# Second block of a fused two-block kernel: every product that GpSimd computes there is given to VectorE

## The chip, the cores and the metric

The kernel runs on one core of one Trainium2 chip, in one launch. The metric is the device time of that launch in microseconds (us). The kernel before took 2101.74 us (median of three runs, 2098.4 to 2101.85).

Names: PE is TensorE (matrix products), DVE is VectorE, ACT is ScalarE, POOL is GpSimd, SP is SyncE, whose queue starts the loads of weights. ACTq and SPq are the queues in which ACT and SP start transfers or wait. "L106" is line 106 of the kernel before.

## The reference, cut to what matters

Two blocks follow each other on 256 tokens of width 2048, all in float32. The change touches the second alone, an RWKV-7 block with a gated short convolution:

```
hn = rmsnorm(concat(16 meta tokens, x));  P = hn @ w_in            # 272 x 2048 @ 2048 x 8320
r, k, v, g_r, wl, al = split(token_shift(P[:, :4224]))              # the recurrent half
Bg, Cg, hc, g_c     = split(P[:, 4224:])                            # the convolution half
a  = sigmoid(a0 + al @ a_lora_up);  decay = exp(-exp(w_raw(wl)))
kk = normalise(k * k_k);  k = k * (1 + (a - 1) * k_a)
y  = recurrence over tokens: S = S diag(decay) - (S kk)(kk*a)^T + v k^T,  y_t = S r_t
y_a = (groupnorm(y) + bonus(r, k, v)) * silu(g_r)
y_b = Bg * causal_conv(Cg * hc) * silu(g_c)
h   = h + concat(y_a, y_b) @ w_out;  out = rmsnorm(h)
```

## The kernel before, in words

**Weights.** All weights (345 MB) are streamed once, in chunks of 128 x 1024 floats (512 KB). A chunk is loaded by SP into one of three tiles `st` (L131). `split` then makes two float32r halves of it: ACT casts it to `wh` (L105), and `wl = st - wh` is computed by DVE or POOL (L106); each half has four tiles. A tile `st` is free for the next load when both halves are done. PE multiplies each chunk three times (hi x hi, hi x lo, lo x hi), so every chunk needs its cast, its subtraction and its PE work in turn. In the second block each third chunk has its subtraction on POOL (`share`, L149 and L150).

**Sections.** In the second block `feat_super` computes 512 features at a time over 16 input tiles, that is 8 chunks (a section); four PSUM accumulators (of six, tile `acc`) take the result. At the end of a section an `evac` function empties the four: DVE reads PSUM (L1095, L193, L1154, L1160), ACT and DVE finish the product. PE may begin the next section in the two accumulators that are left, then needs the emptied ones. The order of sections is k, low-rank inputs, r, v, g, g, then the convolution's Cg, hc, g_c, Bg; then k, r, v and the convolution for the second half of the features; then the output projection (`tok_super`), at first over the part of its inputs that is ready.

**Recurrence.** The generator `rwkv` does the recurrence of one half of the heads by chunks of 64 tokens. Between chunks of weights, `pump` lets it advance by 1.1 credits; each `yield` names what it has used. Its longest part is an elimination that inverts 72 triangular 32 x 32 blocks at once: 31 steps of one product (L1393, into `XT`) and one subtraction (L1397, into `X`) on DVE, one after the other. Then `X` goes to DRAM and comes back in another layout (L1406, L1408, L1413, all started in ACT's queue), and the chunk-by-chunk state update follows (L1509 to L1561), with a group norm (`group_norm`).

**What sets the order.** All engines work in order. A scheduler puts the instructions of each engine in a fixed order when the program is built, by its own estimates of time; a waiting instruction holds up all that stand behind it on its engine.

**What POOL does in the second block before.** Fills with constants (memsets), one small copy (L1338), a third of the subtractions of L106, and these products: gates (L1172, L1173, L1179, L1205), keys (L1256, L1257, L1280), decays (L1316, L1332, L1530) and a row product at the very end (L1659).

Of the kernel before, what the change touches and what calls it, by code (L numbers as in the profile page):

```python
# [9 lines left out]
F32 = mybir.dt.float32  # L10
# [3 lines left out]
ALU = mybir.AluOpType  # L14
AX = mybir.AxisListType

P = 128
D = 2048
S = 256
NM = 16  # L20
# [13 lines left out]
def bc(ap, n):  # L34
    return ap.unsqueeze(len(ap.shape)).to_broadcast(list(ap.shape) + [n])
# [8 lines left out]
def fused_two_blocks(  # L44
# [9 lines left out]
    pe, act, dve, pool = nc.tensor, nc.scalar, nc.vector, nc.gpsimd  # L54
# [18 lines left out]
    queue = []  # L73
# [26 lines left out]
    behind = [None]  # L100
    mm_last = [None]

    def split(hi, lo, src, eng=dve):
        return (
            act.copy(hi, src),  # L105
            eng.tensor_tensor(lo, src, hi.bitcast(F32), ALU.subtract),  # L106
        )

    AHEAD = 3
# [3 lines left out]
    splits = []  # L113
    hold = []
    spare = []
    pos = [0, 0]
# [9 lines left out]
    def load_chunk():  # L126
        w2, k0, nk, c0, ncol = plan[pos[0]]
        pos[0] += 1
        st = wpool.tile([P, WCH], F32, name="st", bufs=3)
        n = nk * ncol  # L130
        nc.sync.dma_start(  # L131
            st[:, :n].rearrange("p (k n) -> p k n", n=ncol),
            w2[k0 * P:(k0 + nk) * P, c0:c0 + ncol].rearrange("(k p) n -> p k n", p=P),
        )
        loaded.append((st[:, :n], ncol))

    def issue_chunk():
        if not loaded:
            load_chunk()
        st, ncol = loaded.pop(0)  # L140
        if spare:
            t = T(spare.pop(0), F32R)
            wh, wl = (t[:, i * WCH:i * WCH + st.shape[1]] for i in range(2))
        else:
            wh, wl = (wpool.tile([P, WCH], F32R, name=name)[:, :st.shape[1]] for name in ("wh", "wl"))
        with ExitStack() as es:
            while hold:
                es.enter_context(tc.issue_after(hold.pop().ins))
            share = behind[0] is not None and queue and pos[0] % 3 == 0  # L149
            splits.append(split(wh, wl, st, pool if share else dve))  # L150
        ready.append(tuple(w.rearrange("p (k n) -> p k n", n=ncol) for w in (wh, wl)))

    def next_chunk(k0, c0, ncol):
# [127 lines left out]
    def T(i, dt=F32):  # L281
        t = tpool.tile([P, 2048], dt, name=f"t{i}")
        return t
# [804 lines left out]
    def x_ops(t0):  # L1088
        return lambda k: xo[:, k, :, t0:]
# [43 lines left out]
    kT = k_proj(0, x_ops0, z_scr)  # L1133
# [7 lines left out]
    mixt = mixpool.tile([P, KT, S], F32, name="mixt")  # L1141
# [7 lines left out]
    def conv_half(hf):  # L1149
        u = rw.tile([P, 4, S + 2], F32, name="u")  # L1150
        n = S + 2

        def ev_c(i, ps):
            dve.tensor_tensor(u[:, i, :], ps, rr3[:, T14:], ALU.mult)  # L1154

        def ev_h(i, ps):
            z = rw.tile([P, L], F32, name="z", bufs=2)
            f = 4 * hf + i
            o = mixt[:, 8 + f, :]
            dve.tensor_tensor(z[:, :n], ps, rr3[:, T14:], ALU.mult)  # L1160
            dve.tensor_tensor(u[:, i, :], u[:, i, :], z[:, :n], ALU.mult)
            act.activation(o, u[:, i, 2:], AF.Copy, scale=pv("conv2", f))
            dve.scalar_tensor_tensor(o, u[:, i, 1:n - 1], pv("conv1", f), o, ALU.mult, ALU.add)
            dve.scalar_tensor_tensor(o, u[:, i, 0:n - 2], pv("conv0", f), o, ALU.mult, ALU.add)

        def ev_g(i, ps):
            z = rw.tile([P, L], F32, name="z", bufs=2)
            g = rw.tile([P, S], F32, name="g", bufs=2)
            o = mixt[:, 8 + 4 * hf + i, :]
            scaled(z[:, :S], ps, rr3[:, NM:])  # L1170
            act.activation(g, z[:, :S], AF.Sigmoid)
            pool.tensor_tensor(g, g, z[:, :S], ALU.mult)  # L1172
            pool.tensor_tensor(o, o, g, ALU.mult)  # L1173

        def ev_b(i, ps):
            g = rw.tile([P, S], F32, name="g", bufs=2)
            o = mixt[:, 8 + 4 * hf + i, :]
            scaled(g, ps, rr3[:, NM:])
            pool.tensor_tensor(o, o, g, ALU.mult)  # L1179

        base = 4224 + 512 * hf
        sec(base + 1024, T14, ev_c)
        sec(base + 2048, T14, ev_h)
        sec(base + 3072, NM, ev_g)
        sec(base, NM, ev_b)

# [12 lines left out]
    def g_proj(hf):  # L1199
        def ev(i, ps):  # L1200
            g = rw.tile([P, S], F32, name="g", bufs=2)
            f = 4 * hf + i
            ev_shift(mixt[:, f, :], 24 + f, ps, T14)
            act.activation(g, mixt[:, f, :], AF.Sigmoid)
            pool.tensor_tensor(mixt[:, f, :], mixt[:, f, :], g, ALU.mult)  # L1205
        sec(3072 + 512 * hf, T14, ev)

    def c64(t, pi):
# [2 lines left out]
    def rwkv(hf, kT, src):  # L1211
        f0 = 4 * hf
        ARm = rw.tile([P, 4, 32], F32, name="ARm")
        BKm = rw.tile([P, 4, 64], F32, name="BKm")
# [4 lines left out]
        aa = r4("a")  # L1219
        for j in range(4):  # L1220
            f = f0 + j
# [8 lines left out]
        kk = r4("kk")  # L1230
        tmp = r4("tmp")
# [14 lines left out]
        ein = r4("ein")  # L1246
# [6 lines left out]
        for j in range(4):  # L1253
            f = f0 + j
            dve.tensor_scalar(tmp[:, j, :], aa[:, j, :], pv("k_a", f), oka[:, f:f + 1], ALU.mult, ALU.add)
        pool.tensor_tensor(kT, kT, tmp, ALU.mult)  # L1256
        pool.tensor_tensor(aa, kk, aa, ALU.mult)  # L1257
        yield 1.3
        AR = rw.tile([P, 2, 4, 2, 2, 64], F32, name="AR")
        BK = rw.tile([P, 2, 4, 2, 2, 64], F32, name="BK")  # L1260
# [15 lines left out]
        for pi in range(2):  # L1276
            dve.tensor_tensor(BK[:, pi, :, :, pi, :], c64(aa[:, :, NM:], pi), c64(nm_, pi), ALU.mult)
            dve.tensor_tensor(BK[:, pi, :, :, 1 - pi, :], c64(kT[:, :, NM:], pi), c64(nm_, pi), ALU.mult)
            if pi == 0:
                pool.tensor_tensor(tmp[:, :, :S], tmp[:, :, :S], kT[:, :, NM:], ALU.mult)  # L1280
            yield 1.3
        dve.tensor_tensor(BKm[:, :, 0:NM], aa[:, :, :NM], eneg[:, :, :NM], ALU.mult)
        dve.tensor_tensor(BKm[:, :, 32:32 + NM], kT[:, :, :NM], eneg[:, :, :NM], ALU.mult)
# [5 lines left out]
        for pi in range(2):  # L1289
            for pp in range(2):  # L1290
                bs = [mix_bank(), mix_bank()]
                for i in range(4):
                    p, cp = 2 * pp + i // 2, i % 2
                    for h in range(2):
                        q = slice(64 * h, 64 * h + 64)
                        pe.matmul(
                            bs[h][:, i * P:(i + 1) * P],
                            BK[q, pi, p, cp].rearrange("p a t -> p (a t)"),
                            AR[q, pi, p, cp].rearrange("p a t -> p (a t)"),
                            start=True, stop=True,  # L1300
                        )
                for h in range(2):
                    dve.tensor_tensor(
                        SS[:, pi, 2 * pp:2 * pp + 2, :, h, :].rearrange("p a c t -> p (a c) t"),
                        bs[h].rearrange("p (a t) -> p a t", t=P), bc_mid(mk[:, pi, :], 4), ALU.mult,
                    )
                yield 1.3
            for g in range(2):
                r0 = 64 * pi + 32 * g
                blk = 16 * (2 * pi + g)  # L1310
                nc.scalar.dma_start(
                    nd[blk:blk + 16].rearrange("b s t -> s b t"),
                    SS[r0:r0 + 32, pi, :, :, :, r0:r0 + 32].rearrange("s p c h t -> s (p c h) t"),
                )

            pool.tensor_tensor(  # L1316
                BK[:, pi].rearrange("p a c s t -> p a c (s t)"), BK[:, pi].rearrange("p a c s t -> p a c (s t)"),
                c64(em, pi)[..., 63:64].to_broadcast([P, 4, 2, P]), ALU.mult,
            )
        for h in range(2):  # L1320
            q = slice(64 * h, 64 * h + 64)
# [7 lines left out]
        nc.scalar.dma_start(nd[64:72].rearrange("b s t -> s b t"), SSm[0:32])  # L1329
        X0 = r4("X0", tag="sw").rearrange("p a t -> p (a t)")[:72, :1024].rearrange("p (s t) -> p s t", t=32)  # L1330
        nc.scalar.dma_start(X0, nd)
        pool.tensor_tensor(BKm, BKm, ein[:, :, NM - 1:NM].to_broadcast([P, 4, 64]), ALU.mult)  # L1332
        decs = rw.tile([P, 4, 4], F32, name="decs")
        dve.tensor_copy(decs, em.rearrange("p a (c t) -> p a c t", t=64)[:, :, :, 63])
        yield 0.7
# [83 lines left out]
        Z = r4("Z", P, tag="kk")  # L1419
        Zd = r4("Zd", P, tag="tmp")  # L1420
# [33 lines left out]
        for i in range(8):  # L1454
            p, h = i // 2, i % 2
            q = slice(64 * h, 64 * h + 64)
# [3 lines left out]
        for h in range(2):  # L1460
            q = slice(64 * h, 64 * h + 64)
# [48 lines left out]
        for c in range(4):  # L1510
            cp, pi = c // 2, c % 2
            a, o = 64 * pi, 64 * (1 - pi)
# [14 lines left out]
            if c < 3:  # L1527
                for h in range(2):
                    q = slice(64 * h, 64 * h + 64)
                    pool.tensor_tensor(Zd[q, :, q], Z[q, :, q], bc(decs[q, :, c], 64), ALU.mult)  # L1530
            if c >= 2:
                next(norm0)
            yield
# [10 lines left out]
            if c < 3:  # L1544
                b4 = mix_bank().rearrange("p (a t) -> p a t", t=P)
                for p in range(4):
                    for h in range(2):
                        q = slice(64 * h, 64 * h + 64)
                        pe.matmul(b4[q, p, q], BKt[:, pi, p, cp, q], UV[:, pi, p, cp, q], start=True, stop=True)
                for h in range(2):  # L1550
                    q = slice(64 * h, 64 * h + 64)
# [33 lines left out]
    for h in range(2):  # L1585
        q = slice(64 * h, 64 * h + 64)
# [5 lines left out]
    for h in range(2):  # L1592
        q = slice(32 * h, 32 * h + 32)
# [7 lines left out]
    for hf in range(2):  # L1601
        if hf == 1:
            kT = k_proj(1, x_ops(0), lambda: None)
            drain()
        src = {}
# [78 lines left out]
    for tb in range(2):  # L1684
        for s in range(2, 4):
            a = acc_bank()
            for k in OUT2_KT:
                if k % 2 == 0 and tb == 0:
                    chunks[s, k] = next_chunk(k, 512 * s, 512)[1]
                wh, wl = (w[:, k % 2, :] for w in chunks[s, k - k % 2])  # L1690
                hi, lo = (mix_ops(k)[:, i, tb * P:(tb + 1) * P] for i in range(2))
# [37 lines left out]
```

## Time and profile before

| | |
|---|---|
| median of three runs | 2101.74 us |
| the profiled execution, its own time | 2102.48 us |
| its span (first to last instruction) | 2100.8 us |
| second block | from about 1485 us of the span to its end |
| PE busy, share of the span | 2050.6 us, 98% |
| DVE, ACT, POOL busy | 1236.1, 1039.0, 323.2 us |
| granted TensorE clock, mean | 0.992 |

Times in rows are us from the start of the span, durations of one instruction are ns. A row that says "idle before <-ACT wh L105" tells how long the engine stood idle in front of such instructions, and what ended the wait. PE's instructions overlap each other, so a stretch in which PE is 100% busy is one without a gap, and the busy times of its groups may not be added up.

### The profile page before, as it was taken

The numbers are of one execution on the slowest core, as the hardware profiler recorded it, in microseconds if no ns is written. First come the engines' busy times: TensorE is split into PE (matmuls) and PEld (weight loads), VectorE is DVE, ScalarE is ACT, GpSimd is POOL, SyncE is SP. The second block draws the span as 40 slices with busy tenths as digits, with TensorE's granted clock in tenths as the row PEclk, the third lists the DMA queues.
The fourth block names the chain that finished last, engine by engine and source line by source line (L and its number), as shares of the span: only waits on it lengthen the run. The fifth ranks groups of instructions, "written<-read, shape, count | busy, mean of one in ns | idle before, by whom it ended". The sixth has DMA issues, their size and how long they took to land.

```text
span 2100.8 us, 29559 instructions
## 1 busy us (share of the span) xinstructions
PE 2050.6 (98%) x11592; PEld 1753.3 (83%) x11592; DVE 1236.1 (59%) x1603; ACT 1039.0 (49%) x1426; POOL 323.2 (15%) x271
## 2 busy tenths in 40 slices
PE   8999999999999999999999999999899999999898
PEld 7898888888888878888888888888798988998686
DVE  6546668654565574444444455565776855668635
ACT  5456566564434464444444454554564434544444
POOL 7002014300011000000000000000034324243422
PEclk9999999999999999999999999999999999999999
DMA  7676654566655566666666655555555553455534
GB/s 223 174 195 184 171 171 141 151 200 192 208 192 180 191 180 192 184 190 190 191 190 189 190 180 187 187 188 190 171 142 167 157 159 104 148 165 165 175 132 141
DMA packets 187884, 369.00 MB, mean 176 GB/s; under 512 B 21229, under 2 KB 29616, under 8 KB 186960
## 3 DMA queue, kind: packets, MB, share of 16 engines
q1 hardware_dynamic: 174752, 352.43, 55.6%
q10 hardware_dynamic: 12016, 11.43, 1.8%
q0 software_dynamic: 976, 3.24, 0.4%
q8 instruction: 91, 1.49, 0.3%
q14 instruction: 49, 0.40, 0.1%
HBM read 361.67 MB, written 5.38 MB: 175 GB/s over the span
## 4 chain that ended last, share of the span: by engine, by line
PE 83%; DVE 8%; DMA 4%; ACT 2%; issue 2%; POOL 1%; ACTq 0%; SPq 0%; DVEq 0%; POOLq 0%
PE acc L221 19%; PE acc L222 19%; PE acc L223 19%; PE acc L177 8%; PE acc L178 4%; PE acc L182 3%; PE acc L183 3%; PE acc L184 3%; DVE wl L106 3%; DMA st<-in_w_in_dram 2%; DVE XT L1393 1%; ACT wh L105 1%; DVE X L1397 1%; PE mx L846 1%; PE mx L714 1%
## 5 line engine op out<-in xcount | busy, mean ns | idle before, releaser
L106 DVE TENSOR_TENSOR wl<-st,wh 128x1024 fp32r<-128x1024 f32 (+1 forms) x626 | 772.4, 1235 | 683.5 <-ACT wh L105 672.6
L105 ACT CAST wh<-st 128x1024 fp32r<-128x1024 f32 (+1 forms) x672 | 699.1, 1042 | 885.7 <-PE acc L222 582.2
L221 PE MATMUL acc<-wh,opnd 128*128 128x512 f32 (+1 forms) x1280 | 498.1, 390 | 4.1 <-ACT opnd L105 4.0
L222 PE MATMUL acc<-wh,opnd 128*128 128x512 f32 (+1 forms) x1280 | 493.4, 386 | 2.2 <-DVE opnd L106 1.7
L223 PE MATMUL acc<-wl,opnd 128*128 128x512 f32 (+1 forms) x1280 | 492.3, 385 | 0.0
L177 PE MATMUL acc<-opnd,wh 128*128 128x512 f32 x896 | 326.7, 406 | 3.2 <-DVE z L193 3.2
L221 PEld LDWEIGHTS acc<-wh,opnd 128*128 128x128 f32 x1280 | 240.8, 188 | 51.0 <-ACT opnd L105 4.2
L222 PEld LDWEIGHTS acc<-wh,opnd 128*128 128x128 f32 x1280 | 241.1, 188 | 48.1 <-DVE opnd L922 2.2
L223 PEld LDWEIGHTS acc<-wl,opnd 128*128 128x128 f32 x1280 | 240.8, 188 | 46.5
L178 PE MATMUL acc<-opnd,wl 128*128 128x256 f32 x896 | 253.0, 282 | 4.6 <-DVE wl L106 4.6
L182 PE MATMUL acc<-opnd,wh 128*128 128x258 f32 (+1 forms) x784 | 225.8, 293 | 4.3 <-DVE z L1095 3.0
L183 PE MATMUL acc<-opnd,wh 128*128 128x258 f32 (+1 forms) x784 | 226.1, 290 | 0.0
L184 PE MATMUL acc<-opnd,wl 128*128 128x258 f32 (+1 forms) x784 | 225.0, 288 | 0.3 <-POOL wl L106 0.3
L177 PEld LDWEIGHTS acc<-opnd,wh 128*128 128x128 f32 x896 | 170.2, 190 | 43.3 <-DVE z L193 3.9
L178 PEld LDWEIGHTS acc<-opnd,wl 128*128 128x128 f32 x896 | 171.0, 191 | 6.1 <-DVE wl L106 5.9
L106 POOL TENSOR_TENSOR wl<-st,wh 128x1024 fp32r<-128x1024 f32 x46 | 118.6, 2578 | 267.2 <-ACT wh L105 244.2
L182 PEld LDWEIGHTS acc<-opnd,wh 128*128 128x128 f32 x784 | 148.5, 191 | 8.8 <-DVE z L1095 3.4
L183 PEld LDWEIGHTS acc<-opnd,wh 128*128 128x128 f32 x784 | 149.7, 191 | 1.6 <-issue 1.4
L184 PEld LDWEIGHTS acc<-opnd,wl 128*128 128x128 f32 x784 | 149.4, 191 | 1.4 <-POOL wl L106 0.5
L221 PE MATMUL acc<-wh,hh 128*128 128x512 f32 x352 | 138.7, 396 | 0.9 <-ACT hh L105 0.9
L222 PE MATMUL acc<-wh,hh 128*128 128x512 f32 x352 | 139.1, 395 | 0.0
L223 PE MATMUL acc<-wl,hh 128*128 128x512 f32 x352 | 138.9, 395 | 0.0
(434 smaller groups left out, 2057.5 us busy)
## 6 DMA issues: line engine op xcount, KB each, us to landing
st<-in_w_in_dram SPq DMA_DIRECT2D x290, 512.0 KB, 3.7
st<-in_w_ffn_in_dram SPq DMA_DIRECT2D x176, 512.0 KB, 3.7
st<-in_w_ffn_down_dram SPq DMA_DIRECT2D x88, 512.0 KB, 3.1
st<-in_w_o_dram SPq DMA_DIRECT2D x32, 512.0 KB, 3.6
st<-in_w_out_dram SPq DMA_DIRECT2D x32, 512.0 KB, 3.6
st<-in_w_in_dram SPq DMA_DIRECT2D x24, 344.0 KB, 3.6
st<-in_w_up_b_dram SPq DMA_DIRECT2D x16, 512.0 KB, 3.7
st<-in_w_up_a_dram SPq DMA_DIRECT2D x16, 512.0 KB, 3.9
```

The source lines that it names most:

```text
L105: act.copy(hi, src),
L106: eng.tensor_tensor(lo, src, hi.bitcast(F32), ALU.subtract),
L177: pe.matmul(av, wh[:, k, m:m + mw], pair, start=first, stop=False)
L178: mm_last[0] = pe.matmul(av[:, 1, :], wl[:, k, m:m + mw], pair[:, 0, :], start=False, stop=last)
L182: pe.matmul(av, wh[:, k, m:m + mw], pair[:, 0, :], start=first, stop=False)
L183: pe.matmul(av, wh[:, k, m:m + mw], pair[:, 1, :], start=False, stop=False)
L184: mm_last[0] = pe.matmul(av, wl[:, k, m:m + mw], pair[:, 0, :], start=False, stop=last)
L221: pe.matmul(a, hi, wk, start=j == 0, stop=False)
L222: pe.matmul(a, lo, wk, start=False, stop=False)
L223: mm_last[0] = pe.matmul(a, hi, wm, start=False, stop=j == nkt - 1)
L714: pe.matmul(b[:, h * P:(h + 1) * P], ke[:, h, ts], qe[:, h, ts], start=True, stop=True)
L846: pe.transpose(b[:, i * P:(i + 1) * P], src[:, i * P:(i + 1) * P], ident)
```

## The change

The argument that let `split` name an engine goes, and with it the rule by which a third of the chunks went to POOL: all subtractions of L106 are DVE's. All products of POOL in the second block but the row product at the end (L1659) go to DVE. In `ev_g` the factors are taken in another order: first z times the convolution's output (into z), then times sigmoid(z), so the first of the two needs no sigmoid. In `rwkv` a `yield 0.6` stands between the two products of the keys. Lines between 150 and 1256 stand one line higher in the changed kernel (its L1204 is L1205 of before, its L1094 is L1095).

```
-    def split(hi, lo, src, eng=dve):
+    def split(hi, lo, src):
...
-            eng.tensor_tensor(lo, src, hi.bitcast(F32), ALU.subtract),
+            dve.tensor_tensor(lo, src, hi.bitcast(F32), ALU.subtract),
...
-            share = behind[0] is not None and queue and pos[0] % 3 == 0
-            splits.append(split(wh, wl, st, pool if share else dve))
+            splits.append(split(wh, wl, st))
...
-            pool.tensor_tensor(g, g, z[:, :S], ALU.mult)
-            pool.tensor_tensor(o, o, g, ALU.mult)
+            dve.tensor_tensor(z[:, :S], z[:, :S], o, ALU.mult)
+            dve.tensor_tensor(o, z[:, :S], g, ALU.mult)
...
-            pool.tensor_tensor(o, o, g, ALU.mult)
+            dve.tensor_tensor(o, o, g, ALU.mult)
...
-            pool.tensor_tensor(mixt[:, f, :], mixt[:, f, :], g, ALU.mult)
+            dve.tensor_tensor(mixt[:, f, :], mixt[:, f, :], g, ALU.mult)
...
-        pool.tensor_tensor(kT, kT, tmp, ALU.mult)
-        pool.tensor_tensor(aa, kk, aa, ALU.mult)
+        dve.tensor_tensor(kT, kT, tmp, ALU.mult)
+        yield 0.6
+        dve.tensor_tensor(aa, kk, aa, ALU.mult)
...
-                pool.tensor_tensor(tmp[:, :, :S], tmp[:, :, :S], kT[:, :, NM:], ALU.mult)
+                dve.tensor_tensor(tmp[:, :, :S], tmp[:, :, :S], kT[:, :, NM:], ALU.mult)
...
-            pool.tensor_tensor(
+            dve.tensor_tensor(
                 BK[:, pi].rearrange("p a c s t -> p a c (s t)"), BK[:, pi].rearrange("p a c s t -> p a c (s t)"),
...
-        pool.tensor_tensor(BKm, BKm, ein[:, :, NM - 1:NM].to_broadcast([P, 4, 64]), ALU.mult)
+        dve.tensor_tensor(BKm, BKm, ein[:, :, NM - 1:NM].to_broadcast([P, 4, 64]), ALU.mult)
...
-                    pool.tensor_tensor(Zd[q, :, q], Z[q, :, q], bc(decs[q, :, c], 64), ALU.mult)
+                    dve.tensor_tensor(Zd[q, :, q], Z[q, :, q], bc(decs[q, :, c], 64), ALU.mult)
```

How it moves instructions, at three places. The first is DVE inside the elimination of the first half, around the emptying of a section of g (`z<-acc` reads PSUM; `mixt` is the gate's tile). Before:

```order
L106 TENSOR_TENSOR wl<-st,wh 128x1024
L1095 TENSOR_TENSOR z<-acc,rr_9807 128x258 x2
L1397 TENSOR_TENSOR X<-X,XT 72x9x23
L1103 SCALAR_TENSOR_TENSOR mixt<-z,pcol,mixt 128x256 x2
L1095 TENSOR_TENSOR z<-acc,rr_9807 128x258 x2
L1393 TENSOR_TENSOR XT<-X,X_13200 72x10x22
L1397 TENSOR_TENSOR X<-X,XT 72x10x22
```

The same place in the change:

```order
L106 TENSOR_TENSOR wl<-st,wh 128x1024
L1094 TENSOR_TENSOR z<-acc,rr_9807 128x258 x2
L1397 TENSOR_TENSOR X<-X,XT 72x7x25
L1102 SCALAR_TENSOR_TENSOR mixt<-z,pcol,mixt 128x256 x2
L1094 TENSOR_TENSOR z<-acc,rr_9807 128x258
L1204 TENSOR_TENSOR mixt<-mixt,g 128x256
L1094 TENSOR_TENSOR z<-acc,rr_9807 128x258
L1393 TENSOR_TENSOR XT<-X,X_13230 72x8x24
L1204 TENSOR_TENSOR mixt<-mixt,g 128x256
L1397 TENSOR_TENSOR X<-X,XT 72x8x24
L1102 SCALAR_TENSOR_TENSOR mixt<-z,pcol,mixt 128x256 x2
L106 TENSOR_TENSOR wl<-st,wh 128x1024
```

The four gate products stand among the steps of the elimination and between the reads of PSUM, and a subtraction of L106 follows where POOL took it before; the elimination is two steps less far at this section's end.

The second place is DVE at the end of section v of the first half. Before, in front of the first read of PSUM and up to the second:

```order
L1272 TENSOR_TENSOR AR<-r,ein 128x8x64
L1277 TENSOR_TENSOR BK<-a,sw 128x8x64
L1278 TENSOR_TENSOR BK<-k,sw 128x8x64
L106 TENSOR_TENSOR wl<-st,wh 128x1024 x2
L1095 TENSOR_TENSOR z<-acc,rr_9807 128x272
L106 TENSOR_TENSOR wl<-st,wh 128x1024
L1099 SCALAR_TENSOR_TENSOR v<-z,pcol,v 128x271
L1095 TENSOR_TENSOR z<-acc,rr_9807 128x272 x2
```

In the change:

```order
L1265 TENSOR_TENSOR AR<-kk,ein 128x8x63
L1266 COPY AR<-kk 128x8
L106 TENSOR_TENSOR wl<-st,wh 128x1024 x5
L1094 TENSOR_TENSOR z<-acc,rr_9807 128x272
L106 TENSOR_TENSOR wl<-st,wh 128x1024
L1098 SCALAR_TENSOR_TENSOR v<-z,pcol,v 128x271
L1094 TENSOR_TENSOR z<-acc,rr_9807 128x272 x2
```

The products of r (L1272) and of the keys (L1277, L1278) have moved behind this section, and five subtractions in a row stand in front of the first read of PSUM; between the first and the second read there is one subtraction, as before.

The third place is ACT at the change from the last section to the output projection (`opnd` is the projection's left operand, `xd` the elimination's result in DRAM). Before:

```order
L1406 DMA xd<-X 72x1024
L105 CAST wh<-st 128x1024
L1408 DMA TTm<-xd 32x8x32
L1413 DMA TT<-xd 32x16x32 x4
L105 CAST wh<-st 128x1024 x2
L192 COPY g<-acc 128x256 x2
L105 CAST wh<-st 128x1024
L105 CAST opnd<-mixt 128x2x256
```

In the change:

```order
L1406 DMA xd<-X 72x1024
L105 CAST wh<-st 128x1024
L191 COPY g<-acc 128x256
L1408 DMA TTm<-xd 32x8x32
L1413 DMA TT<-xd 32x16x32 x4
L191 COPY g<-acc 128x256 x2
L105 CAST wh<-st 128x1024
L105 CAST opnd<-mixt 128x2x256
```

Two casts of weights no longer stand between the five transfers and the first `opnd`, and the first read of PSUM stands in front of them. SP's order is the same in both. POOL keeps its memsets, the copy of L1338, one transfer and the five row products of L1659 from here on; PE's order moves by up to one chunk at some steps of the recurrence.

## Rows read from the trace of the kernel before

**Rows 1.** The page: the span, and its first part (engine, busy us, share, instructions).
```profile
span 2100.8 us, 29559 instructions
PE 2050.6 (98%) x11592; PEld 1753.3 (83%) x11592; DVE 1236.1 (59%) x1603; ACT 1039.0 (49%) x1426; POOL 323.2 (15%) x271
```

**Rows 2.** Waits of PE from 1495 us: total us, times, longest us.
```profile
PE acc L178 <- DVE wl L106: 4.6, 4, 2.2
PE acc L221 <- ACT opnd L105: 4.0, 1, 4.0
PE acc L182 <- DVE z L1095: 3.0, 2, 2.2
PE mx L1495 <- DVE Y L1491: 2.0, 1, 2.0
PE acc L222 <- DVE opnd L106: 1.7, 1, 1.7
PE acc L177 <- DVE z L193: 1.2, 1, 1.2
PE mx L1296 <- DVE SS L1303: 1.2, 1, 1.2
PE acc L184 <- POOL wl L106: 0.3, 1, 0.3
```

**Rows 3.** Stretches: length, busy PE, PEld, DVE, ACT, POOL, PEclk, DMA share, GB/s.
```profile
1495.00:2100.80 605.80, 576.91 (x4476) 526.20 (x4474) 391.20 (x596) 290.31 (x423) 199.75 (x132) 0.98 0.50 151
1636.50:1686.30 49.80, 49.64 (x417) 49.43 (x416) 46.71 (x84) 22.81 (x32) 18.47 (x12) 1.00 0.47 141
1903.30:1961.90 58.60, 53.51 (x335) 47.35 (x334) 54.92 (x96) 26.74 (x38) 23.07 (x15) 1.00 0.44 140
1710.00:1760.00 50.00, 48.94 (x479) 41.94 (x478) 18.98 (x26) 23.40 (x36) 18.13 (x17) 0.93 0.40 125
1777.00:1780.40 3.40, 3.40 (x30) 3.40 (x29) 2.98 (x2) 0.34 (x1) 3.37 (x3) 1.00 0.18 69
1618.40:1621.80 3.40, 3.40 (x18) 3.40 (x18) 2.17 (x4) 0.68 (x1) 0.35 (x1) 0.50 0.77 187
1785.70:1789.10 3.40, 3.40 (x17) 3.40 (x16) 1.71 (x3) 1.51 (x4) 0.00 (x0) 0.50 0.81 257
1973.40:1983.60 10.20, 8.05 (x59) 6.49 (x60) 9.51 (x15) 4.73 (x9) 5.40 (x5) 0.50 0.66 208
```

**Rows 4.** Groups of POOL from 1495 us: busy us, mean ns, idle before.
```profile
L106 POOL TENSOR_TENSOR wl<-st,wh 128x1024 fp32r<-128x1024 f32 x46 | 118.6, 2578 | 267.2 <-ACT wh L105 244.2 <-PE mx L1296 16.8 <-PE acc L184 6.1
```

**Rows 5.** Groups of DVE, from 1495 us.
```profile
L106 DVE TENSOR_TENSOR wl<-st,wh 128x1024 fp32r<-128x1024 f32 x112 | 146.3, 1308 | 100.1 <-ACT wh L105 99.5 <-PE acc L183 0.3
L1393 DVE TENSOR_TENSOR XT<-X,X 72x31 f32<-72x31 f32 (+15 forms) x62 | 36.6, 591 | 3.1 <-DMA X<-nd 1.6
L1397 DVE TENSOR_TENSOR X<-X,XT 72x31 f32<-72x31 f32 (+15 forms) x62 | 28.4, 458 | 1.8
L1397 DVE TENSOR_TENSOR X<-X,XT 72x192 f32<-72x192 f32 x4 | 1.4, 352 | 0.1
```

**Rows 6.** The subtraction on DVE in the first block, 1100 to 1480 us.
```profile
L106 DVE TENSOR_TENSOR wl<-st,wh 128x1024 fp32r<-128x1024 f32 x135 | 165.5, 1226 | 175.6 <-ACT wh L105 175.2
```

**Rows 7.** Single lines: shortest, median and longest ns, first and last start.
```profile
L198 DVE TENSOR_TENSOR z<-z,rr x24: 411/420/1947, 179.7 to 1950.8; 128x256 f32<-128x256 f32 x24
...
L1303 DVE TENSOR_TENSOR SS<-mx,mk x16: 677/682/692, 1608.2 to 1891.5; 128x512 f32<-128x512 f32 x16
```

**Rows 8.** Timeline of POOL, then of DVE, in the second elimination: start us, duration us.
```profile
1931.68 3.05 POOL L106 TENSOR_TENSOR wl<-st,wh 128x1024 fp32r<-128x1024 f32 x1 [5.10 <-ACT wh L105]
...
1932.40 2.62 DVE L1393 TENSOR_TENSOR XT<-X,X 72x255 f32<-72x255 f32 x1
1935.05 0.42 DVE L1397 TENSOR_TENSOR X<-X,XT 72x255 f32<-72x255 f32 x1
```

**Rows 9.** The chain that ended last, after the second elimination: start us, us, what.
```profile
1961.87 5.30 DMA xd<-X
```

## The prediction, made before the change was timed

> **What bounds the kernel now.** First the page: PE is busy in 2050.6 of 2100.8 us, DVE in 59%, POOL in 15% [rows 1]. So the time is PE's work and its gaps, and this change alters no matrix product: it can only take gaps away or add some. The order of DVE is the same until the first half's recurrence begins, and POOL takes no chunk before it, so the first block and the start of the second stay. Second, the waits of PE from 1495 us on, which tell who ended its gaps [rows 2]. Four of them are for a low half that DVE made late (4.6 us), two for a read of PSUM at the end of a section (3.0), one each for the group norm (2.0), for z in L193 (1.2), for a masked product (1.2) and for a low half of POOL (0.3): 12.3 us. Two more, 4.0 and 1.7 us, stand where the output projection begins. Third, the same time by stretches [rows 3]: after PE has stood still the granted clock falls to 0.50, that is the 1.2 GHz level, and the stretch at 1618.4 shows 18 matmuls begun in 3.4 us where 3.4 us at 1.00, the 2.4 GHz level, hold 30. The one at 1785.7, behind the wait for the group norm, holds 17. That is 12/30 of 3.4 us, 1.4 us, for each. At 1973.4 the clock is low for 10.2 us.
>
> **Why DVE is late.** The reader is to look at a product of POOL and one of DVE side by side [rows 8]. POOL begins a low half at 1931.68 and ends at 1934.73; DVE begins a step of the elimination at 1932.40 and needs 2.62 us for it, until 1935.02; the next step, of the same size, takes 0.42. So DVE did nothing until POOL was done. The same in sums: the 124 steps of the two eliminations take 36.6 + 28.4 = 65.0 us [rows 5]. A step of 192 elements, a little over the mean size of 176, takes 0.352 us; 124 of these are 43.6, so 21.4 us are waiting inside instructions. A product of 256 elements takes 0.42 us in the median and 1.95 at worst, whereas the 16 products of L1303, which read PSUM, all lie between 677 and 692 ns [rows 7].
>
> By the Trainium skill ("SBUF — State Buffer", section "SBUF: two separate sides") VectorE and GpSimd hold a shared pair of ports as an exclusive lock, if the VectorE instruction has two SBUF inputs and the GpSimd one reads SBUF: the later one stands still until the earlier ends. The trace agrees: 2.62 us beside 0.42, and 677 to 692 ns for the form with one PSUM input.
>
> **The change, part by part.** (1) 46 low halves leave POOL, where one takes 2.578 us [rows 4], and go to DVE, where one takes 1.226 us when POOL is idle [rows 6]: 56.4 us more on DVE. (2) The other products are 199.75 - 118.6 = 81 us of POOL at most, the memsets and the row product at the end included [rows 3, 4]; at the same ratio, 2578/1226 = 2.10, they would be at most 39 us on DVE. (3) Gone from DVE is what it waits for POOL inside instructions: at least the 21.4 us of the eliminations and 112 x (1.308 - 1.226) = 9.2 us in its own low halves [rows 5, 6], 30.6 us; at most all 199.75 us in which POOL is busy. DVE's load in the 606 us so goes from 391 to between 286 and 456 us (391 - 199.75 + 95 and 391 - 30.6 + 95). That is a mean and decides nothing.
>
> What decides are the two stretches in which DVE is full, the eliminations: 46.71 of 49.8 us and 54.92 of 58.6 us [rows 3]. POOL is busy there for 18.47 and 23.07 us, which as work of DVE is 8.8 and 11.0 us. Half of the 21.4 us, 10.7, comes back in each as the least, and 18.5 and 23.1 as the most. The first then has between 46.7 + 8.8 - 18.5 = 37.0 and 44.8 us of 49.8, the second between 42.8 and 55.2 us of 58.6. I take the middle, 41 and 49, because rows 8 show the whole overlap returned. So DVE gets about 5 to 6 us of room in each. Elsewhere it has room already: in the stretch from 1710 us it is busy for 19 of 50 us, and 18.1 us of POOL would add 8.6.
>
> (4) The gaps. The low halves that were late, the reads of PSUM behind them, the group norm, the masked product and POOL's late half: 12.3 us. I count them as gone, since each stands behind a DVE instruction that was stretched or queued behind one; the bounds are 0 and 12.3. With them go the two stretches of half clock behind such gaps, 2.7 us. A low half that ends earlier also frees its tile `st`, so loads start earlier.
>
> (5) The change to the projection: 4.0 + 1.7 us, and 0.4 x 8.05 = 3.2 us for the low clock there, 8.9 us. The first `opnd` stands in ACT's queue behind the transfers of the elimination's result, which come 5.30 us after its last step [rows 9]. If DVE ends the elimination some 5 us earlier, these transfers are over earlier, and the order has two casts fewer in front. But in the change a read of the last section's PSUM (L192) stands ahead of the transfers, and the lower half of `opnd` waits on DVE behind four gates' work. I take half, 4.5, between 0 and 8.9.
>
> (6) What is added in waits. 45 or 46 low halves now wait in DVE's queue for ACT's cast. On DVE such a wait is 100.1/112 = 0.89 us each [rows 5], so about 41 us more of standing still; in the eliminations, with some 9 of these halves, 8 us, in the 18 us that are free there (9 of 50, 10 of 59). Behind each stand the steps of the elimination and the reads of PSUM that free an accumulator. The gates now wait in DVE's queue for a sigmoid of ACT; L1316 waits there for PE. Before, two of 15 section ends cost PE 3.0 us, 1.5 us each [rows 2]. Bounds for the new gaps: nothing, and 15 x 1.5 = 22.5 us. I take 5, near three ends, since most section ends had a low half between the reads of PSUM before too and cost nothing. The `yield 0.6` moves the recurrence by less than a chunk, work that lies beside PE's; I price it at 0.
>
> Sum: 12.3 + 2.7 + 4.5 - 5 = 14.5 us. The profiled execution took 2102.5 us, 0.7 above the median, so 2088 us.
>
> **Rivals.** *A. The low halves stay late.* In the eliminations all of them now queue between steps, where POOL took every third at once. Then the 4.6 us of L178 and the gain at the projection stay away: 14.5 - 4.6 - 4.5 = 5.4 us, 2097 us. For it: DVE is still over 80% busy in these stretches. Against: it was 94%.
>
> *B. Other waits take the place of all.* PE then stands for loads and casts: DVE waits 99.5 us for casts as it is [rows 5]. About 2101 us. Against: no row of PE's waits names a load.
>
> *C. DVE becomes the bound, slower.* If only part of the waiting inside instructions comes back, the second elimination needs 54.9 + 11.0 us less what returns. It decides from the point where less than 7.3 us returns (65.9 - 58.6), or where the added 41 us of standing fall into the eliminations and section ends. At section ends the price is 1.5 us each at 15 ends, 22.5 us, against 12.3 + 2.7 gained less the 3.0 of the section ends, 12.0: 2102.5 + 10.5 = 2113 us. For it: the engine that is fullest gets more instructions, all in one in-order queue. Against: 10.7 us is the least that rows 5 give back.
>
> By the Trainium skill ("Perfetto Trace Analysis", section "Optimizing Scalar/DVE Operations"), work of a saturated VectorE may be handed to GpSimd, which speaks for C; the same place warns that the two share a read port, so that this may not help. At 94% and with 2.62 us beside 0.42 the trace bears out the warning.
>
> *D. It does not do what it says:* the order shows POOL without products until the end, so 2 in 100 at most; its time would be 2102.
>
> **How the numbers follow.** About 0.2%, 4.2 us, can be told from no change here: under 2097.5 counts as faster than the median of 2101.7, over 2106 as slower. Forecast 66%, with a range of its own from 2078.6 (everything of 23.9 us gone, nothing new) to 2096 (new gaps of 13 us). A 14%, B 7%, C 11%, D 2%. Faster: forecast and A, 0.80; same: B and D, 0.09; slower: C, 0.11. The range 2078 to 2102 leaves out C and a few in a hundred below.
>
> **What would show it.** Right: L1393 and L1397 close to 44 us for all 124; no DVE product of two SBUF inputs over its shortest by more than 0.2 us outside the last 60 us; L106 on DVE at 1.2 us in the second block; the PE waits for L106, L1095, L1491 and L1303 together under 5 us; the half-clock stretches behind 1615 and 1783 us gone. Step 5 is right if PE's wait for `opnd` halves. Wrong: a PE wait for z, SS or u at more than four section ends (C), or L178 waiting for L106 as before (A). If POOL's products did not hold DVE up, the steps would stay at 0.59 and 0.46 us in the mean.

## The result, and the profile after

The changed kernel takes 2078.35 us (median of four runs, 2076.09 to 2080.55) against 2101.8 us of the kernel before in the same comparison: ratio 0.9886, 95% interval 0.9871 to 0.9901. It is faster by 23.4 us where 14.5 were forecast. First the page, which answers [rows 1]:

```profile
span 2076.6 us, 29533 instructions
PE 2043.8 (98%) x11592; PEld 1748.3 (84%) x11592; DVE 1249.3 (60%) x1705; ACT 1038.8 (50%) x1426; POOL 138.3 (7%) x169
```

DVE got 102 more instructions and is busy for only 13 us more: most of what it took over replaces time in which it had stood still inside its instructions. PE is busy for 6.8 us less, though no product changed; the low clock below accounts for 6.4 of them. The groups of DVE from 1490 us on, beside [rows 5]:

```profile
L106 DVE TENSOR_TENSOR wl<-st,wh 128x1024 fp32r<-128x1024 f32 x158 | 193.5, 1227 | 107.7 <-ACT wh L105 106.9 <-PE acc L176 0.3
L1397 DVE TENSOR_TENSOR X<-X,XT 72x31 f32<-72x31 f32 (+15 forms) x62 | 20.9, 337 | 1.5
L1393 DVE TENSOR_TENSOR XT<-X,X 72x31 f32<-72x31 f32 (+15 forms) x62 | 20.9, 337 | 5.3 <-DMA X<-nd 4.0
```

The 124 steps of the eliminations take 41.8 us for 65.0 before. Counted over all of DVE from 1490 to 2030 us, as what each instruction takes above the shortest of its form in any run, the time held inside instructions falls from about 68 us to about 1. Next the waits of PE from 1495 us on, all there are, beside [rows 2]:

```profile
PE acc L220 <- ACT opnd L105: 2.0, 1, 2.0
PE acc L221 <- DVE opnd L106: 1.7, 1, 1.7
PE acc L176 <- DVE z L192: 0.9, 1, 0.9
PE acc L181 <- ACT opnd L920: 0.7, 1, 0.7
PE mx L1222 <- ACT sw L1223: 0.2, 1, 0.2
```

Before, four more rows than [rows 2] shows stood in that list, and there were two more stretches at 0.50, at 1717.4 and 1724.2 us, which the prediction did not use:

```profile
PE mx L1457 <- ACT UVm L1439: 1.1, 1, 1.1
PE acc L182 <- ACT opnd L921: 0.7, 1, 0.7
...
PE acc L182 <- DVE u L1154: 0.2, 1, 0.2
PE mx L1223 <- ACT sw L1224: 0.2, 1, 0.2
```

```profile
1717.40:1720.80 3.40, 3.40 (x12) 2.78 (x11) 0.00 (x0) 0.45 (x1) 1.67 (x3) 0.50 0.73 235
1724.20:1727.60 3.40, 3.40 (x12) 2.92 (x12) 0.00 (x0) 0.59 (x1) 0.00 (x0) 0.50 0.54 154
```

The kernel after, by stretches (length, busy PE, PEld, DVE, ACT, POOL, PEclk, DMA share, GB/s), beside [rows 3]: the second block, the two eliminations, the stretch at 1618.4 us, and the two that now run at the 1.2 GHz level between 1500 and 2060 us:

```profile
1490.00:2076.60 586.60, 572.02 (x4487) 523.16 (x4487) 408.58 (x707) 292.84 (x427) 16.41 (x30) 0.98 0.52 158
1631.90:1675.70 43.80, 43.80 (x369) 43.80 (x368) 41.38 (x92) 22.52 (x33) 1.58 (x3) 1.00 0.56 161
1889.60:1941.50 51.90, 50.99 (x317) 45.28 (x316) 48.91 (x111) 28.06 (x40) 0.96 (x1) 1.00 0.53 166
1618.40:1621.80 3.40, 3.40 (x37) 3.28 (x36) 2.60 (x4) 0.77 (x1) 0.00 (x0) 1.00 0.65 179
1712.70:1716.10 3.40, 3.40 (x12) 2.83 (x12) 0.00 (x0) 0.43 (x1) 0.00 (x0) 0.50 0.49 150
1951.60:1958.40 6.80, 5.41 (x13) 4.25 (x14) 5.64 (x11) 3.78 (x7) 0.00 (x0) 0.50 0.63 218
```

The eliminations last 43.8 and 51.9 us for 49.8 and 58.6, and DVE is still busy for 94% of each: they end earlier, they did not become empty. Between 1500 and 2060 us the clock is low for 3.4 + 6.8 = 10.2 us, before for 4 x 3.4 + 10.2 = 23.8. In the two long stretches PE also stands still, so of these times it is busy for 8.8 us now and for 21.65 before; at half speed the difference costs 6.4 us, an estimate. With the waits, 20.2 us before and 5.5 now, it makes 21.1 of the 24.2 us between the spans. Not every low stretch stands behind a wait: PE is busy for all of the 4.7 us before 1712.7 in the kernel after, with 77 products at 1.00.

Where the 24.2 us went can be read by laying the same matrix product of both profiled executions side by side (its start before less its start after, and how much that grows in each stretch of the time before): up to 1490 us 0.7, which is chance, since the instructions are the same; end of the v section, to 1589 us, 3.7; masked products and the low clock behind, to 1642 us, 3.1; first elimination and what follows, to 1710 us, 1.5; state update, to 1760 us, 2.7; group norm and the low clock behind, to 1800 us, 3.7; on to 1903 us 2.1; second elimination, to 1964 us, 3.8; the output projection 2.2; the end 0.7. So 15.3 us came outside the eliminations and what directly follows them: 3.7 + 3.1 + 2.7 + 3.7 + 2.1. The group norm's part is the plainest. Before, a low half of POOL ran beside a small DVE instruction of the norm, early in the chain to the result for which PE then waited 2.0 us [rows 2, L1495]:

```profile
1777.97 2.40 POOL L106 TENSOR_TENSOR wl<-st,wh 128x1024 fp32r<-128x1024 f32 x1
1778.10 2.30 DVE L1484 TENSOR_SCALAR ls<-ls 128x8 f32<-128x8 f32 x1
```

In the kernel after none of the four instructions of L1484 takes more than 0.173 us.

### The profile page after: what moved, and what is told of

Read it like the earlier page. It is cut to its first block, busy times and chain, and to the rows that moved or that the text cites. A ratio compares the mean times of both kernels' runs of the same rounds, so it can differ in the third digit from the quotient of the medians.

```text
span 2076.6 us, 29533 instructions
## 1 busy us (share of the span) xinstructions
PE 2043.8 (98%) x11592; PEld 1748.3 (84%) x11592; DVE 1249.3 (60%) x1705; ACT 1038.8 (50%) x1426; POOL 138.3 (7%) x169
## 4 chain that ended last, share of the span: by engine, by line
PE 91%; DVE 3%; DMA 2%; ACT 2%; issue 1%; POOL 1%; SPq 0%; ACTq 0%; DVEq 0%; POOLq 0%
PE acc L220 19%; PE acc L221 19%; PE acc L222 19%; PE acc L176 8%; PE acc L181 5%; PE acc L182 5%; PE acc L183 4%; PE acc L177 4%; DVE wl L106 1%; PE mx L845 1%; PE mx L713 1%; ACT wh L105 1%; DMA st<-in_w_in_dram 1%; PE mx L1296 0%; PE mx L1539 0%
## 5 line engine op out<-in xcount | busy, mean ns | idle before, releaser
L106 DVE TENSOR_TENSOR wl<-st,wh 128x1024 fp32r<-128x1024 f32 (+1 forms) x672 | 819.7, 1221 | 690.9 <-ACT wh L105 685.4
L220 PEld LDWEIGHTS acc<-wh,hh 128*128 128x128 f32 x352 | 65.9, 187 | 17.1 <-ACT hh L105 1.0
```

The costliest lines, as they stand in the source:

```text
L106: dve.tensor_tensor(lo, src, hi.bitcast(F32), ALU.subtract),
L220: pe.matmul(a, hi, wk, start=j == 0, stop=False)
```

## The experiments

Theory 1: GpSimd's products hold VectorE inside its instructions, and the gain is the end of that. Theory 2: what GpSimd made came late by itself. Theory 3: the new order, or the added `yield 0.6`. Each kernel ran in five rounds beside the kernel before (medians 2101.2 to 2102.0 us); its difference to the kernel after goes by the two ratios.

**One part at a time.** Only the low halves moved (the kernel before, `split` always on DVE):

```
-            splits.append(split(wh, wl, st, pool if share else dve))
+            splits.append(split(wh, wl, st))
```

> The kernel before, with the 46 low halves on VectorE alone; every other product stays on GpSimd. Theory 1 (the gain is the time in which GpSimd's products hold VectorE's two-input instructions): the low halves are 118.6 of the 199.75 us of GpSimd's products, so about 59% of the 23.4 us: 2088, between 2084 and 2092; VectorE's subtractions of the line near 1.23 us, the remaining masked products still up to 2.6 us long. Theory 2 (the gain is that results made by GpSimd itself come late on the way to TensorE): of TensorE's waits before only 0.3 us named a low half of GpSimd, so at most 3 us: 2098 to 2102. Theory 3 (the new order and the added 0.6 of the planner): nothing of it is in here, 2100 to 2103.

Only the products moved (the kernel after, with `share` and `split(wh, wl, st, pool if share else dve)` as before):

> The kernel after, with every third low half back on GpSimd; all other products on VectorE, the added 0.6 of the planner kept. Theory 1: the remaining 41% of the gain, 2092, between 2088 and 2096; VectorE's subtractions near 1.6 us again beside GpSimd's. Theory 2: nearly all of the gain, 2078 to 2082. Theory 3: all of it, 2077 to 2080.

Measured: 2084.67 us, ratio 0.9915 (0.9903 to 0.9928), and 2084.8 us, 0.9924 (0.9911 to 0.9937). Each part alone brings 16 to 18 of the 23.4 us, together they bring less than the sum. Theory 3 falls for the first kernel: it has neither the `yield` nor the new order of factors in `ev_g`, and all but some 40 of DVE's 1603 instructions stand in the order of before. Theory 2 falls as the whole: it allowed the first at most 3 us. My shares by busy time, 59 and 41%, fell too: the end of the first half's v section gives 3.3 us in both, so there either part alone was enough to end the wait.

The second kernel gains its 16 us although its steps are hardly shorter than before, 60.7 us for 65.0:

```profile
L1398 DVE TENSOR_TENSOR X<-X,XT 72x31 f32<-72x31 f32 (+15 forms) x62 | 33.3, 537 | 1.8
L1394 DVE TENSOR_TENSOR XT<-X,X 72x31 f32<-72x31 f32 (+15 forms) x62 | 27.4, 442 | 5.8 <-DMA X<-nd 4.3
```

So the steps alone do not tell the time. GpSimd takes ten low halves in its eliminations, 10 x 1.23 = 12.3 us that VectorE has not to do there; 18.9 us more in steps than in the kernel after, less these 12.3, leave 6.6 us, and it is 6.5 us slower than the kernel after by the medians. How much of what the products bring is the end of their hold, and how much that their own results came late, is not separated: before, ScalarE waited 12.2 us for such results in the second block and TensorE 0.3, in the kernel after both not at all.

**The hold alone.** The kernel after, plus products on GpSimd whose results nobody uses (`scrap` is a part of `mixt` not yet written, and from the second half's convolution on the tile `wlu`):

```
             splits.append(split(wh, wl, st))
+            if share and scrap:
+                n = st.shape[1]
+                pool.tensor_tensor(scrap[0][:, :n], wh.bitcast(F32), wh.bitcast(F32), ALU.mult)
```

> The kernel after, plus 42 products on GpSimd of 128x1024 that read the high half just made and write a scrap area: nobody uses them, they begin where GpSimd's low halves began before (four in the output projection are left out). VectorE keeps all of its own work. Theory 1: the holds come back while VectorE also carries the low halves, so at least the low halves' share of the gain is lost: 2090 to 2104; VectorE's masked products and subtractions up to 2.6 and 2.9 us long where one lies beside. Theories 2 and 3: nobody waits for these products and the order of the rest is the same, 2076 to 2081.

The control has, in place of the product, a copy of one column and two fills:

```
+                pool.tensor_copy(scrap[0][:, :1], wh.bitcast(F32)[:, :1])
+                pool.memset(scrap[0][:, :n], 0.0)
+                pool.memset(scrap[0][:, :n], 1.0)
```

> As the run with 42 products that nobody uses, but each is a copy of one element a row and two constant fills of 128x1024 (about 2 us together) on GpSimd. Theory 1, in the form that only a GpSimd instruction that reads data holds VectorE: 2076 to 2081, and no two-input VectorE instruction longer than in the kernel after. Rival (any GpSimd instruction that writes there holds it): about as slow as with the products, 2088 to 2100. Theories 2 and 3: 2076 to 2081.

Measured: 2092.19 us, 0.9958 (0.9942 to 0.9974), with the products, of which the trace has 39; 2079.8 us, 0.9895 (0.9882 to 0.9908), with the fills. The groups of DVE and POOL, first with the products:

```profile
L106 DVE TENSOR_TENSOR wl<-st,wh 128x1024 fp32r<-128x1024 f32 x158 | 205.7, 1304 | 84.1 <-ACT wh L105 82.7 <-PE acc L188 0.9
L154 POOL TENSOR_TENSOR mixt<-wh 128x1024 f32<-128x1024 f32 x28 | 70.6, 2523 | 195.8 <-ACT wh L105 190.1 <-ACT v L1103 5.7
L154 POOL TENSOR_TENSOR wlu<-wh 128x1024 f32<-128x1024 f32 x11 | 28.4, 2584 | 75.0 <-ACT wh L105 75.0
L1399 DVE TENSOR_TENSOR XT<-X,X 72x31 f32<-72x31 f32 (+15 forms) x62 | 27.5, 444 | 2.0 <-DMA X<-nd 0.6
L1403 DVE TENSOR_TENSOR X<-X,XT 72x31 f32<-72x31 f32 (+15 forms) x62 | 27.1, 437 | 1.5
```

and with the fills:

```profile
L106 DVE TENSOR_TENSOR wl<-st,wh 128x1024 fp32r<-128x1024 f32 x158 | 193.4, 1226 | 106.7 <-ACT wh L105 105.3 <-PE mx L853 0.7
L156 POOL MEMSET mixt<- 128x1024 f32 x28 | 26.8, 957 | 1.5
L1405 DVE TENSOR_TENSOR X<-X,XT 72x31 f32<-72x31 f32 (+15 forms) x62 | 20.9, 337 | 1.5
L1401 DVE TENSOR_TENSOR XT<-X,X 72x31 f32<-72x31 f32 (+15 forms) x62 | 20.9, 337 | 6.0 <-DMA X<-nd 4.6
```

Products that read data and whose results nobody uses stretch the steps from 41.8 to 54.6 us and DVE's low halves from 1227 to 1304 ns, and cost 15 us (0.9958 less 0.9886, times 2102). Fills of about 2 us in the same places leave the steps at 41.8 and cost 2 us, which is not told apart from nothing. TensorE, VectorE and ScalarE have the same instructions in the same order in the two kernels, so the order does not explain the difference. Nor do the tiles that GpSimd occupies: ScalarE waits for these for 4.8 us with the products and for 7.2 with the fills. That is the hold by itself, without late results.

**All of it back, and the places.** To the idle products one each is added for the gates, key products and decays, for instance:

```
             dve.tensor_tensor(mixt[:, f, :], mixt[:, f, :], g, ALU.mult)
+            pool.tensor_tensor(scrap[0][:, :S], g, g, ALU.mult)
```

> As the run with 42 products that nobody uses, plus one on GpSimd for each of the other products that moved (gates, key products, decays), of the same size and at the place where GpSimd had them; two small ones per half and four low halves in the output projection are left out. VectorE does all the real work. Theory 1 (holding VectorE is the whole of it): VectorE is held as before the change and carries some 90 us more, so all of the gain is gone: 2099 to 2112. Theory 2 for the part that the 42 left (what they didn't bring back is the lateness of results that GpSimd made itself): nobody waits for these either, so 2089 to 2094, as with the 42.

Then only those idle products that are issued between the first and the last step of an elimination (`if share and scrap and elim[0]`):

> The kernel after, plus only those of the 42 unused products that fall into the two eliminations: 10 of them. Theory 1 with its place in the eliminations (VectorE is loaded to about four fifths there and has no room to catch up): most of the 12.5 us that the 42 cost against the kernel after, 2084 to 2090. If the holds cost the same everywhere, 10/42 of it: 3 us, 2080 to 2083. Theories 2 and 3: 2076 to 2081.

Measured: 2114.79 us, 1.0067 (1.0052 to 1.0081), and 2091.39 us, 0.9949 (0.9938 to 0.9961). The first is slower than before: VectorE with the work and the hold is the state in which rival C put the kernel. It is not the hold alone, though: the added products also read tiles that ScalarE fills anew, and the chain of work that ended last runs through four of them for 6.8 us at 1948 to 1955 us. The waits of PE in it, from 1495 us on, the five largest:

```profile
PE acc L226 <- ACT x L105: 13.7, 1, 13.7
PE acc L187 <- DVE u L1159: 4.6, 1, 4.6
PE acc L189 <- DVE wl L106: 4.1, 4, 1.6
PE acc L182 <- DVE z L198: 3.8, 1, 3.8
PE mx L1309 <- DVE SS L1316: 2.9, 3, 1.6
```

The second is the sharpest for the place: ten products cost 13 us, nearly as much as 39 (15). One of them on POOL's timeline (start us, duration us), and the DVE step that it holds:

```profile
1921.63 1.90 POOL L155 TENSOR_TENSOR wlu<-wh 128x1024 f32<-128x1024 f32 x1 [4.27 <-ACT wh L105]
```

```profile
1921.79 2.01 DVE L1405 TENSOR_TENSOR X<-X,XT 72x255 f32<-72x255 f32 x1
```

A step of this size takes 0.42 us in the kernel after. Its two groups of steps:

```profile
L1405 DVE TENSOR_TENSOR X<-X,XT 72x31 f32<-72x31 f32 (+15 forms) x62 | 27.1, 437 | 1.5
L1401 DVE TENSOR_TENSOR XT<-X,X 72x31 f32<-72x31 f32 (+15 forms) x62 | 25.8, 416 | 3.4 <-DMA X<-nd 2.1
```

52.9 less 41.8 is 11.1 us inside steps. Not all of the 13 us is its price. The last of the ten is waited for after all: the projection's first operand lies in the place of `wlu`, and ScalarE stands for 3.0 us until that product is done. And of the 13.1 us between the profiled executions of this kernel and the kernel after, 2.8 lie before 1490 us, where both do the same. That leaves 7 to 10 us, an estimate: in the eliminations a microsecond of hold costs most of one of the kernel, and the other 29 products, outside them, hardly anything.

**From the other side.** The kernel before with no low half on POOL in the eliminations, and the kernel after with low halves on POOL outside them:

```
-            share = behind[0] is not None and queue and pos[0] % 3 == 0
+            share = behind[0] is not None and queue and pos[0] % 3 == 0 and not elim[0]
```

> The kernel before, with one thing changed: the 8 low halves that GpSimd took during the two eliminations go to VectorE; the other 38 and all other products stay on GpSimd. By the run with 10 unused products in the eliminations (they cost as much as 42), the holds matter in the eliminations: half of the low halves' gain of 17 us or more from these 8, 2090 to 2095. If every low half counts the same: 8/46 of 17 us, 3 us, 2097 to 2100. Waits at the ends of sections, which lie outside the eliminations, stay in either case.

> The kernel after, with every third low half back on GpSimd except in the eliminations: 36 of 46. If holds cost only where VectorE has no room: within 2 us of the kernel after, 2077 to 2081. If they cost everywhere: 36/46 of the 6.5 us by which the kernel with only the products moved is slower than after: 2083 to 2086.

Measured: 2096.46 us, 0.9978 (0.9967 to 0.9989), and 2079.79 us, 0.9896 (0.9881 to 0.9911). The second agrees: POOL's 36 low halves cost nothing that can be told from noise, though outside the eliminations they still hold DVE for about 27 us, counted as above. Its groups:

```profile
L106 POOL TENSOR_TENSOR wl<-st,wh 128x1024 fp32r<-128x1024 f32 x36 | 89.3, 2481 | 325.1 <-ACT wh L105 275.1 <-PE mx L1543 25.3 <-PE mx L1298 20.6
L1400 DVE TENSOR_TENSOR X<-X,XT 72x31 f32<-72x31 f32 (+15 forms) x62 | 20.9, 337 | 1.5
L1396 DVE TENSOR_TENSOR XT<-X,X 72x31 f32<-72x31 f32 (+15 forms) x62 | 20.9, 337 | 5.3 <-DMA X<-nd 4.0
```

The first is between the two expectations: 4.6 us (2.3 to 6.9) where 3 or 7 to 12 were expected. Its steps fell from 65.0 to 51.5 us:

```profile
L1395 DVE TENSOR_TENSOR XT<-X,X 72x31 f32<-72x31 f32 (+15 forms) x62 | 26.5, 427 | 2.8 <-DMA X<-nd 1.3
L1399 DVE TENSOR_TENSOR X<-X,XT 72x31 f32<-72x31 f32 (+15 forms) x62 | 25.0, 403 | 1.9
```

But the eight low halves are now VectorE's own work there, 8 x 1.23 = 9.8 us, so of the 13.5 us 3.7 are net, near the 4.6 gained. The waits outside stayed: 2.8 us for z, 2.0 for the group norm, 1.2 for a masked product.

**The order.** The kernel after without the line `yield 0.6`:

> The kernel after without the added 0.6 of the planner between the two key products. Theory 3 (the spacing is part of the gain): two products of 1.22 us stand in a row again and TensorE's transposes behind them come late, 2081 to 2086. Theories 1 and 2: the step moves some instructions by one load and nothing else, 2076 to 2081.

2079.97 us, 0.9895 (0.9881 to 0.9908): not told apart from the kernel after. Theory 3 falls for the `yield`; the new order of factors in `ev_g` was not run by itself.

**What is left.** The transfers of the elimination's result issued by GpSimd (`nc.scalar.dma_start` becomes `nc.gpsimd.dma_start` for `xd`, `TTm` and `TT`), then the same with a third `yield 3.2` ahead of their first reader:

> The kernel after with the six transfers of each elimination's result (the one out of X and the five back) issued from GpSimd instead of ScalarE. In the kernel after ScalarE stands between 1943.3 and 1948.3 us behind them (it waits for the first to land, then issues five), while the section's end and the operands' high halves wait for it; TensorE then waits 2.0 and 1.7 us and runs 6.8 us at the lower clock (3.4 us lost). If that is the cause: 2071 to 2075. If the waits have another cause, or GpSimd's issues come as late for the elimination's own chain: 2076 to 2082. Theory 1 says nothing on it, except that these issues, which read no data through VectorE's side, must not lengthen VectorE's instructions.

> The run with the elimination's six result transfers on GpSimd, plus one more pause of 3.2 in the planner before their first reader: there the operands no longer came late, but TensorE waited 2.8 us for the transfer to TTm, which landed 4.4 us after its issue instead of 3.2. If only that wait stands between it and its gain: 2073 to 2076 against 2078 of the kernel after. If the pause pushes the second half's state update into the last product: 2077 to 2080.

2076.18 us, 0.9876 (0.986 to 0.9891), and 2077.53 us, 0.9883 (0.9869 to 0.9897): neither is told apart from the kernel after. PE's waits of the first, from 1495 us on:

```profile
PE mx L1436 <- DMA TTm<-xd: 2.8, 1, 2.8
PE acc L176 <- DVE z L192: 1.6, 1, 1.6
PE acc L181 <- ACT opnd L920: 0.7, 1, 0.7
PE mx L1222 <- ACT sw L1223: 0.2, 1, 0.2
```

The waits for `opnd` are gone, so ACT's issues did cause them; a wait for the slower transfer took their place (landing 4.4 us after the issue, 3.2 from ACT). With the pause `opnd` is waited for again, 2.5 and 1.0 us, for a cause that I did not follow. No version here beats the kernel after beyond the noise.

## Why the prediction was right in direction and short in size

- *The mechanism held.* That POOL's products hold DVE up is shown by the idle products and their control. Of step (3), "at least" 30.6 and "at most" 199.75 us, about 67 us came back. The steps take 41.8 us (about 44 said), a low half 1227 ns (1.2 us said). Steps (1) and (2), 95 us more on DVE at most: DVE's busy time from 1490 us on is 409 us, inside the 286 to 456 us given. The loads taken for the eliminations, 41 and 49 us, came out as 41.4 and 48.9. But the "5 to 6 us of room in each" did not come: the stretches became shorter by 6.0 and 6.7 us and stayed 94% full. And the hold reaches further than the two SBUF inputs that the prediction asked for: L1484, above, has one.
- *Step (4), the gaps,* held: of 12.3 us 11.4 are gone (0.9 us for z is left). The stretch at 1618.4 now starts 37 products at 1.00 where 18 began at 0.50, and the one behind the group norm is gone. At half speed they were worth 1.7 us each, not 1.4, an estimate from 18 against 37.
- *Step (5), the projection,* taken as 4.5: the waits for `opnd` fell from 5.7 to 3.7 us, not by half, and PE's busy time at the low clock there from 8.05 to 5.41 us, 1.3 us at half speed. Together 3.3, near the size taken. What kept the rest is shown by the run that moved the transfers: ACT stood in its own queue of issues there.
- *Step (6) failed.* "I take 5, near three ends" was the mis-sized term of the sum: new waits cost 0. The five rows of after are all there are, and each stood in the list of before, at the same place of the kernel and as long or longer. I had set 41 us more of standing for casts against the room in a full engine. DVE hardly stands longer for them: 106.9 us for 158 low halves, where it stood 99.5 us for 112 [rows 5], 7 us more.
- *Not priced:* the waits for UVm and u, 1.3 us, and the second of the two low stretches at 1717 and 1724 us, 1.7 us. The sum as measured is 11.4 + 3.4 + 3.3 + 0 + 3.0 = 21.1 us; of the remaining 3.1 us of span 0.7 lies before the second block, and the rest is not assigned. So it is in part luck that the time came out beside the bound of 2078.6 us for "everything of 23.9 us gone, nothing new": step (5) brought 3.3 of its 8.9 us, and terms that the sum did not have made up for it.
- *The rivals.* A fell: PE waits no longer for a low half of L106 in the second block. B fell: no row names a load. C did not happen, but what it describes exists: with the hold kept and the work moved the kernel takes 2114.79 us. That this is near C's 2113 is luck: TensorE's largest wait there is for the projection's first operand (13.7 us), not for section ends. D fell with the page.

## What to carry to other kernels

Compare an instruction's mean with its shortest time before counting an engine's busy share as work: 65.0 us of steps were 41.8 of work. Work handed to GpSimd that reads SBUF is paid by VectorE where VectorE is full: set the time that it holds VectorE there against the work that it takes off it (18.9 against 12.3 us in one run, and the kernel was 6.5 us slower). Where VectorE has room it can be free, as the 36 low halves were, unless the hold falls on an instruction that TensorE is about to wait for, as the group norm's 2.30 us did before. So hand it over by place, not by every third chunk. When an in-order engine is freed of such holds, do not add a charge for its new waits without a row that shows where they would end last: here the charge was 5 us and the waits cost nothing.

## What the runs showed of the hardware

The hold goes both ways. In the control GpSimd's copy of one element a row reads data too, and this line shows its shortest, median and longest time in ns:

```profile
L154 POOL COPY mixt<-wh x28: 185/1171/2257, 1540.2 to 1836.6; 128x1 f32<-128x1 f32 x28
```

It does 185 ns of work and takes 1171 in the median. ACT's cast releases both it and DVE's subtraction; where the subtraction begins first, as by 0.10 us at 1552.1 us, the copy ends 0.04 us behind it, and where the copy begins first, as at 1628.4 us, it takes 0.19 us. By the Trainium skill ("SBUF — State Buffer", section "SBUF: two separate sides") the later of the two stands until the earlier ends, whichever began first; the trace agrees for both engines, and the fills, which read nothing, held no step (337 ns in the mean). They did hold four instructions of VectorE that have one tensor as input: two of the eight of L1262 take 0.92 and 0.94 us beside a fill, the other six 0.40 to 0.42.
